# A two-layer diffusion backbone on one core: layer 1's modulation and gate sums four at a time on column groups of TensorE, taps and small vectors laid out by the host

## The chip, the cores and the metric

The kernel runs on one core of one Trainium2 chip (trn2). The metric is the device time of one execution in microseconds. Before the change three runs gave 1686.88, 1685.45 and 1686.14 us; their median is 1686.14.

The engines are named as the profile names them: PE is TensorE (PEld its weight loads), DVE VectorE, ACT ScalarE, POOL GpSimd, SP SyncE, which issues nearly all DMAs. PSUM is the memory that PE writes its results to.

## The reference, cut to what matters

The program is a trunk of two layers over 1024 latent tokens and 256 context tokens of 1024 channels. Layer 0 is windowed attention (16 heads of 128, four key heads), layer 1 a convolution module (a depthwise convolution of 31 taps over 2048 channels between two projections). Both layers are modulated by a conditioning vector `c`:

```python
for i in range(DEPTH):
    shift, scale, gate = jnp.split((silu_c @ ada_w[i] + ada_b[i])[:, None, :], 3, axis=-1)
    h_lat = modulate(rmsnorm(x, norm_g[i]), shift, scale)      # h * (1 + scale) + shift
    ...
    x = x + gate * y                                           # y: attention or convolution branch
return rmsnorm(x, final_g)
```

`silu_c @ ada_w[i]` is a product of one row of 1024 with a matrix of 1024 x 3072. Layer 0's shift and scale are needed at the very start. Layer 0's gate is needed when the attention's output projection ends, layer 1's shift and scale just behind that, layer 1's gate at the end of the kernel. The change touches these four pieces of 1024 values (called chunks of 256 below), and how the depthwise taps `conv_dw_w` (31 x 2048), the biases and the norm weights come into the layout of one channel per partition.

## The kernel before, in words

All large products are made from float32 values split into a high and a low part (`Hh`/`Hl`, `whi`/`wlo`), three matmuls for one product. Weights come as raw tiles of 128 columns (`wraw`), ACT copies the high part, POOL or DVE subtracts it to get the low part.

**Stages.** A start (to about 60 us) loads x, normalizes it, makes layer 0's shift and scale (`ada_mm`, `ada_row`, `ada_cols`, lines 402 to 430) and projects the first key, query and value chunk. The heads follow: a loop over 16 heads x 8 blocks of 128 queries (line 1280). One step computes the scores of the next block, does twelve matmuls of the projections as filler (`fill`), and transposes the probabilities of the present block on PE (`transposes`, line 1119), four or five 128x128 transpositions; every four blocks the product with the values follows. Then come layer 0's output projection, layer 1's projections with the convolution beside them on DVE, ACT and POOL, the layer norm, and layer 1's output projection.

**What sets the order.** PE's instructions are kept in the order in which the program is written (`pin`, line 106 and 1260); the other engines' instructions are put in order by a scheduler that simulates the program. SP's queue of DMAs is one of these: a DMA that waits for its target holds up those behind it.

**The modulation that this change touches** is `ada_rest` (lines 665 to 702), a generator that the head loop advances once a step (line 1327). It has 16 chunks of 256 columns: four of layer 0's gate, eight of layer 1's shift and scale, four of layer 1's gate. For each chunk it takes eight steps, in each of which DVE multiplies a raw 128x256 tile of weights by a column of `silu(c)` and adds it to `acc` in PSUM (the bias comes in as a diagonal, `ident` times a column of `abt`). After the eighth, DVE copies `acc` to `acc_a`, a quarter of the mask's page. One step later PE sums over the 128 partitions: for a gate chunk one fp32 matmul of `ones[:, 0:1]` with `acc_a` (a row of 256, copied by DVE and stored to DRAM, `gd`), for a shift or scale chunk two fp32 matmuls of `acc_a` with a column of ones (two columns of 128, copied to `mod1`). The raw tiles alternate between two places that the taps `dww` and their pair sums `wsum` take later (line 652).

**Taps and small vectors.** `k_rows` (line 173) holds `c`, `c_ctx`, a norm weight and layer 0's biases as 48 rows of 128; PE transposes them once (line 334), and from the result ACT makes `cs = silu(c)`. `k_vecs` holds 128 such rows of biases and norm weights, transposed by `turn_vecs` (line 512) within the first projection. The taps are loaded as two tiles of 31 rows (`dwr`, line 1351) and turned by 16 small transpositions in four calls of `turn_taps` (line 1356), which stand first in the list `later` and are done in the first two steps of layer 0's output projection; the last call sums the taps by pairs (`sum_taps`).

**Pages.** Nearly all SBUF tiles come from a pool of 45 pages of 4 KB per partition (line 115), each freed page going to the end of the list of free ones and each allocation taking the first (lines 54 to 76). A tile in a page waits until the page's last reader is done. `WStream` (line 214) loads and splits the raw weights in such pages: `split` gives up the raw page, and the next `load` follows.

Of the kernel before, what the change touches and what calls it, by code (L numbers as in the profile page):

```python
# [9 lines left out]
F32 = mybir.dt.float32  # L10
# [84 lines left out]
def backbone_kernel(  # L95
    ctx_stack: ExitStack,
    tc: tile.TileContext,
    x, ctx, ada_w, attn_sink, attn_w_out, conv_dw_w, conv_w_out, final_g,
    k_rows, k_vecs, k_ada, k_win, k_wconv, k_xt,
    k_cos, k_sin, k_mask, k_ident,  # L100
    out,
):
# [9 lines left out]
    hfpool = ctx_stack.enter_context(tc.tile_pool(name="halves", bufs=1))  # L112
    ps = ctx_stack.enter_context(tc.tile_pool(name="ps", bufs=2, space=PSUM))
    dr = ctx_stack.enter_context(tc.tile_pool(name="dr", bufs=1, space=bass.MemoryType.DRAM))
    pg = Pages(pgpool, 45, "page", 1024)
    hp = Pages(hfpool, 6, "half", 528)

    uid = [0]
# [10 lines left out]
    def ps_o(i=None):  # L129
        if i is None:  # L130
            oflip[0] ^= 1
            i = oflip[0]
        return ps.tile([P, 512], F32, tag=f"o{i}", name=nm("pso"), bufs=1)

    def ps_g():
        return ps.tile([P, 512], F32, tag="g", name=nm("psg"), bufs=2)
# [13 lines left out]
    def act(out, in_, func, **kw):  # L150
        return A.activation(out=out, in_=in_, func=func, **kw)
# [18 lines left out]
    ptlo = ctile([P, 22, P], F32R, "ptlo")  # L170

    crow_pg = hp.alloc(F32, None, "crow")
    crow = crow_pg[0:48, 0:P]
    SY.dma_start(out=crow, in_=k_rows)
    SY.dma_start(out=idsel, in_=k_ident)
    G.memset(ones, 1.0)
# [153 lines left out]
        ada_load(kt)  # L330

    cs = ctile([P, 40], F32, "cs")[:, 0:16]
    tp = ps_g()
    PE.transpose(tp[:, 0:48], crow, ident[0:48, 0:48])
    act(cs, tp[:, 0:16], AF.Silu)
    V.tensor_copy(vt[:, 96:112], tp[:, 16:32])
    bcol = ctile([P, 16], F32, "bcol")
    V.tensor_copy(bcol[:, 0:8], tp[:, 32:40])
    V.tensor_scalar(out=bcol[:, 8:16], in0=tp[:, 40:48], scalar1=1.0, scalar2=None, op0=ALU.add)
    hp.free(crow_pg)  # L340
    xs1 = load_rows(x[0, 512:768], 2)
    ada_load(6)
    xs1 += load_rows(x[0, 768:1024], 2)
    ada_load(7)
    cx = load_rows(ctx[0], 2)
    vec_pg = pg.alloc(F32, [P], "vecs")
    SY.dma_start(out=vec_pg, in_=k_vecs)
    xt1 = [pg.alloc(F32, [2, 512], "xt") for _ in range(4)]
    for i in range(4):
        SY.dma_start(out=xt1[i], in_=k_xt[i])  # L350
# [158 lines left out]
                PE.matmul(acc[n], w[p // 2][:, kt], (Hl if p == 1 else Hh)[kt][:, sl],  # L509
                          start=kt == 0 and p == 0, stop=kt == KT - 1 and p == 2)  # L510

    def turn_vecs():
        tp = ps_o()
        PE.transpose(tp[:, 0:P], vec_pg, ident)
        V.tensor_copy(vt[:, 0:96], tp[:, 0:96])
        V.tensor_copy(abt, tp[:, 96:P])
        pg.free(vec_pg)

    abt = ctile([P, 32], F32, "abt")

    sa, sb = ps_s(), ps_s()
    acc0 = [t[:, i * 512:i * 512 + 512] for t, i in ((sb, 0), (sb, 1), (sa, 0))]

# [49 lines left out]
    for kt in range(2, KT):  # L573
        nx = kt + 1
        if 2 < kt < KT - 1:
            ada_row(nx)
            tp = turn(xs0, nx, ps_g) if nx < KT - 1 else turn_apart(xs0[0:2], nx, ps_g())
        if kt == 5:
            root1 = rstd_root(ss1, D, 4)
        if kt == KT - 1:  # L580
            x_mm(kt - 1, 0, acc0, (2,))
            turn_vecs()
            for n in (2, 0, 1):
                x_mm(kt, 0, acc0, (n,), (0,))
        x_mm(kt, 0, acc0, (0,), {2: (0,), KT - 1: (1, 2)}.get(kt, range(3)))
        if nx == KT - 1:
            tp = tp, turn_apart(xs0[2:4], nx, ps_o(0))
        if nx < KT:
            ada_cols(nx)
            if kt == 5:  # L590
                r1 = rstd_end(root1, 4)
            if nx < KT - 1:
                x_tile(tp, nx, 0, V)
            else:
                x_tile_apart(tp, nx)
        else:
            x_h(0)
            x_f(1)
            x_l(0)
            rc = rstd_end(rootc, 2)  # L600
        if kt == 2:
            x_mm(kt, 0, acc0, (0,), (1, 2))
        if nx < KT:
            x_mm(kt, 0, acc0, (1,))
            x_mm(kt - 1, 0, acc0, (2,), range(3) if kt > 2 else (2,))
        else:
            x_mm(kt, 0, acc0, (2, 1), (1, 2))
        for i in {3: (0, 1), 4: (2, 3)}.get(kt, ()):
            square(xs1[i], ss1[:, i:i + 1], A)
        if kt == 4:  # L610
            pg.free(*xs1)
        if kt == 5:
            rps = ps_o(1)
            for b in range(4):
                PE.matmul(rps[:, b * P:b * P + P], r1[:, b:b + 1].to_broadcast([P, P]), ident, start=True, stop=True)
            rb_pg = pg.alloc(F32, [1024], "rb")
            rb1 = rb_pg[:, 0:512]
            act(rb1, rps, AF.Copy)
            for i in range(2):
                square(cx[i], ssc[:, i:i + 1], A)  # L620
        if kt == 6:
            pg.free(*xs0)
            cos, sin = (pg.alloc(F32, [1024], n) for n in ("cos", "sin"))
            SY.dma_start(out=cos, in_=k_cos)
            SY.dma_start(out=sin, in_=k_sin)
            rootc = rstd_root(ssc, D, 2)
            x_f(0)
# [20 lines left out]

    gd = [dr.tile([1, D], F32, tag=f"gd{i}", name=f"gd{i}") for i in range(2)]
    mod1 = ctile([P, 16], F32, "mod1")  # L650
    acc_a = mask_pg[:, 768:1024]
    ada_raw = [cpool.tile([P, n], F32, tag=t, name=t + "_raw", bufs=1)[:, 0:256]
               for t, n in (("dww", NJ * TAPS), ("wsum", NJ * 16))]

# [10 lines left out]
    def ada_rest():  # L665
        todo = [(l, c0) for l, c0 in [(0, 2048 + 256 * i) for i in range(4)] + [(1, 256 * i) for i in range(12)]]
        todo = [(l, c0, kt) for l, c0 in todo for kt in range(KT)]

        def load(i):
            l, c0, kt = todo[i]  # L670
            SY.dma_start(out=ada_raw[i % 2], in_=ada_w[l, kt * P:(kt + 1) * P, c0:c0 + 256])

        load(0)
        bank = ps_o(1)
        acc, o = bank[:, 0:256], bank[:, 256:512]
        for i, (l, c0, kt) in enumerate(todo):
            if i + 1 < len(todo):
                load(i + 1)
            raw = ada_raw[i % 2]
            if kt == 0:  # L680
                after(V.tensor_scalar(out=acc, in0=raw, scalar1=cs[:, kt:kt + 1], scalar2=None, op0=ALU.mult))
                for b in range(2):
                    col = (c0 - 2048 if l == 0 else 1024 + c0) // P + b
                    bs = slice(b * P, b * P + P)
                    stt(acc[:, bs], ident, abt[:, col:col + 1], acc[:, bs], ALU.mult, ALU.add)
            else:
                after(stt(acc, raw, cs[:, kt:kt + 1], acc, ALU.mult, ALU.add))
            yield
            if kt < KT - 1:
                continue  # L690
            V.tensor_copy(acc_a, acc)
            yield "copied"
            if i + 1 == len(todo):
                yield
            if c0 >= 2048:
                PE.matmul(o[0:1], ones[:, 0:1], acc_a, start=True, stop=True)
                V.tensor_copy(acc_a[0:1], o[0:1])
                SY.dma_start(out=gd[l][:, c0 - 2048:c0 - 1792], in_=acc_a[0:1])
            else:
                for b in range(2):  # L700
                    PE.matmul(o[:, b:b + 1], acc_a[:, b * P:b * P + P], ones[:, 0:1], start=True, stop=True)
                V.tensor_copy(mod1[:, c0 // P:c0 // P + 2], o[:, 0:2])

    adag = ada_rest()

# [642 lines left out]
    gbc0.append(gate_rows(0))  # L1348


    dwr = pg.alloc(F32, [1024], "dwr"), pg.alloc(F32, [1024], "dwr")
    for i in range(2):
        G.memset(dwr[i][0:32, :], 0.0)
        SY.dma_start(out=dwr[i][0:TAPS, :], in_=conv_dw_w[0, :, i * 1024:(i + 1) * 1024])

    def turn_taps(q):
        o = ps_o()
        for i in range(4):
            j = q * 4 + i
            PE.transpose(o[:, i * 32:(i + 1) * 32], dwr[j // 8][0:32, (j % 8) * P:(j % 8 + 1) * P], ident[0:32, 0:32])  # L1360
        V.tensor_copy(dww[:, q * 4:q * 4 + 4, :], o[:, 0:128].rearrange("p (a b) -> p a b", b=32)[:, :, 0:TAPS])
        if q == 3:
            pg.free(*dwr)
            sum_taps()

    for q in range(4):
        later.append(lambda q=q: turn_taps(q))


    border = []  # L1370
# [573 lines left out]
def _laid_out(i):  # L1944
    rows = [i["c"], i["c_ctx"], i["norm_g"], i["ada_b"][0, 0:2 * D]]
    vecs = [i["conv_b_in"], i["conv_dw_b"], i["conv_ln_g"], i["conv_ln_b"], i["ada_b"][0, 2 * D:], i["ada_b"][1]]
    ada = i["ada_w"][0, :, 0:2 * D].reshape(2, 4, P, 2, KT, P).transpose(4, 0, 2, 1, 3, 5).reshape(KT, 2, P, 4, 2 * P)
    return {"k_rows": np.concatenate([v.reshape(-1, P) for v in rows]),
            "k_vecs": np.concatenate([v.reshape(-1, P) for v in vecs]),
            "k_ada": ada, "k_win": _columns(i["attn_w_in"][0]), "k_wconv": _columns(i["conv_w_in"][0]),  # L1950
            "k_xt": i["x"][0, 512:].reshape(512, 4, 2, P).transpose(1, 3, 2, 0)}


_INS = ["x", "ctx", "ada_w", "attn_sink", "attn_w_out", "conv_dw_w", "conv_w_out", "final_g"]
_OUTS = [((1, T, D), "float32")]


# [18 lines left out]
```

## Time and profile before

| | before |
|---|---|
| median of three runs | 1686.14 us (1685.45 to 1686.88) |
| span of the profiled execution, first to last instruction | 1684.8 us |
| difference between that span and the median (what lies around it) | 1.3 us |
| PE busy, matmul records | 1675.0 us, 8436 |
| DVE, ACT, POOL busy | 1116.1, 878.8, 871.0 us |
| mean clock granted to TensorE | 0.999 |

The profiled execution's own device time is not listed apart from its span, so sums are made against the span and carried to the median.

How to read it: a line of a timeline gives start, duration, engine, line, operation, output and inputs, sizes and count. Since every instruction goes through one helper, nearly all have the line L89, and tiles tell them apart. The records of PE overlap: the start of one record to the start of the next is the turn that it took, its duration is the time until its result is out. A plain fp32 matmul leaves two records, a transposition or a matmul of rounded fp32 one. An idle time in square brackets stands before the work and names what ended it.

### The profile page before, as it was taken

How to read it: one execution, taken by the hardware profiler on the slowest of the kernel's cores; microseconds unless marked ns; L12 is line 12 of the kernel's file. 1: busy time of each engine (PE TensorE's matmuls, PEld its weight loads, DVE VectorE, ACT ScalarE, POOL GpSimd, SP SyncE). 2: the span in 40 equal slices, each digit the busy share in tenths (PEclk: the TensorE clock that was granted, in tenths of full speed). 3: DMA queues.
4: the chain of work that ended last, by engine and by line, in shares of the span. 5: the costliest groups of instructions: out<-in, count | busy, mean ns of one | idle time of the engine just before them, and what ended most of it. 6: DMA issues, size and time to landing. Idle time of an engine off the chain costs nothing.

```text
span 1684.8 us, 23963 instructions
## 1 busy us (share of the span) xinstructions
PE 1675.0 (99%) x8436; PEld 1413.9 (84%) x8436; DVE 1116.1 (66%) x2131; ACT 878.8 (52%) x1555; POOL 871.0 (52%) x722
## 2 busy tenths in 40 slices
PE   9999999999999999999999999999999999999998
PEld 6888888888888888888888888888888888888886
DVE  5765654566356644566324289999999999868732
ACT  5745543555355543556334365555665654566741
POOL 0256653666366663653001267999898888130400
PEclk9999999999999999999999999999999999999999
DMA  9424443454244443447976522020211202387881
GB/s 387 150 85 153 134 121 95 153 153 141 84 152 144 143 135 98 135 135 251 320 233 228 213 94 91 11 72 17 75 51 51 82 33 80 130 276 241 310 298 50
DMA packets 114776, 244.55 MB, mean 145 GB/s; under 512 B 11626, under 2 KB 36514, under 8 KB 114656
## 3 DMA queue, kind: packets, MB, share of 16 engines
q1 hardware_dynamic: 108576, 233.06, 40.9%
q10 hardware_dynamic: 6080, 9.97, 2.4%
q8 instruction: 66, 1.08, 0.3%
q14 instruction: 54, 0.44, 0.1%
HBM read 190.80 MB, written 41.69 MB: 138 GB/s over the span
## 4 chain that ended last, share of the span: by engine, by line
PE 98%; DVE 0%; DMA 0%; ACT 0%; POOL 0%; issue 0%; ACTq 0%; POOLq 0%
PE psg L89 51%; PE pss L89 26%; PE pso L89 22%; DMA rope_half<-rope_half 0%; POOL rope_half L89 0%; DVE x_page L89 0%; ACT p_page L89 0%; DVE wlo_page L89 0%; ACT pthi L89 0%; ACT rope_half L89 0%; ACT whi_page L89 0%; DVE hf_page L89 0%; DVE hl_page L89 0%; ACT qh_page L89 0%; ACT lhi_page L89 0%
## 5 line engine op out<-in xcount | busy, mean ns | idle before, releaser
L89 POOL TENSOR_TENSOR odd_half<-odd_half,prod_half 128x513 f32<-128x513 f32 (+2 forms) x252 | 314.7, 1257 | 22.6 <-ACT prod_half L89 9.4
L89 POOL TENSOR_TENSOR wlo_page<-wraw_page,whi_page 128x512 fp32r<-128x512 f32 (+1 forms) x104 | 173.0, 1680 | 186.7 <-DVE ql_page L89 72.0
L89 PE MATMUL psg<-hh_page,whi_page 128*128 128x512 f32 x600 | 236.3, 394 | 0.0
L89 PE MATMUL psg<-hl_page,whi_page 128*128 128x512 f32 x600 | 234.4, 391 | 0.0
L89 PE MATMUL psg<-hh_page,wlo_page 128*128 128x512 f32 x600 | 234.0, 390 | 0.0
L89 ACT ACTIVATE prod_half<-ubuf,dww 128x513 f32<-128x513 f32 (+2 forms) x252 | 165.6, 675 | 116.9 <-POOL odd_half L89 113.0
L89 PE MATMUL psg<-h2h_page,whi_page 128*128 128x512 f32 x464 | 181.9, 392 | 0.0
L89 PE MATMUL psg<-h2h_page,wlo_page 128*128 128x512 f32 x464 | 180.6, 389 | 0.0
L89 PE MATMUL psg<-h2l_page,whi_page 128*128 128x512 f32 x464 | 180.6, 389 | 0.0
L89 POOL TENSOR_SCALAR p_page<-p_page,sc 128x640 f32<-128x640 f32 (+1 forms) x128 | 99.6, 779 | 149.5 <-DVE sc L89 131.8
L89 DVE SCALAR_TENSOR_TENSOR pss<-ubuf,dww,pss 128x512 f32<-128x512 f32 (+3 forms) x270 | 172.4, 670 | 0.1
L89 DVE SCALAR_TENSOR_TENSOR pss<-ubuf,wsum,pss 128x512 f32<-128x512 f32 (+3 forms) x270 | 171.7, 671 | 0.2
L89 ACT ACTIVATE p_page<-p_page,sc 128x641 f32<-128x641 f32 (+1 forms) x128 | 102.9, 804 | 98.3 <-DVE sc L89 95.9
L89 ACT ACTIVATE pthi<-pss 128x512 fp32r<-128x512 f32 (+2 forms) x144 | 87.3, 618 | 109.7 <-PE pss L89 99.8
L89 DVE TENSOR_TENSOR ptlo<-pss,pthi 128x512 fp32r<-128x512 f32 (+2 forms) x144 | 101.8, 716 | 61.2 <-ACT pthi L89 59.9
L89 PEld LDWEIGHTS psg<-hh_page,wlo_page 128*128 128x128 f32 x600 | 112.7, 188 | 24.3
L89 PEld LDWEIGHTS psg<-hh_page,whi_page 128*128 128x128 f32 x600 | 112.8, 188 | 19.2 <-ACT hh_page L89 0.3
L89 PEld LDWEIGHTS psg<-hl_page,whi_page 128*128 128x128 f32 x600 | 112.8, 188 | 18.4
L89 ACT ACTIVATE whi_page<-wraw_page 128x1024 fp32r<-128x1024 f32 x88 | 92.6, 1052 | 49.8 <-PE psg L89 21.1
L89 PE MATMUL pso<-h2h_page,whi_page 128*128 128x512 f32 x304 | 118.3, 389 | 0.0
L89 PE MATMUL pso<-h2h_page,wlo_page 128*128 128x512 f32 x304 | 118.3, 389 | 0.0
L89 PE MATMUL pso<-h2l_page,whi_page 128*128 128x512 f32 x304 | 118.3, 389 | 0.0
(262 smaller groups left out, 3992.4 us busy)
## 6 DMA issues: line engine op xcount, KB each, us to landing
wraw_page<-in_k_wconv_dram SPq DMA_DIRECT2D x48, 512.0 KB, 3.3
wraw_page<-in_k_win_dram SPq DMA_DIRECT2D x40, 512.0 KB, 3.6
wo_page<-in_attn_w_out_dram SPq DMA_DIRECT2D x32, 512.0 KB, 6.2
wol_page<-wolA SPq DMA_DIRECT2D x32, 512.0 KB, 8.3
wo_page<-in_conv_w_out_dram SPq DMA_DIRECT2D x32, 512.0 KB, 6.7
wol_page<-wolC SPq DMA_DIRECT2D x32, 512.0 KB, 6.2
rope_half<-rope_half ACTq DMA_DIRECT2D x76, 128.0 KB, 2.4
araw_page<-in_k_ada_dram SPq DMA_DIRECT2D x16, 512.0 KB, 10.1
```

The source lines that it names most:

```text
L89: r = f(*a, **k)
```

## The change

- `k_rows` and `k_vecs` are turned by the host, so that a partition holds one channel: `crow` is loaded as 128 x 48 and used as it is, `vt[:, 0:96]` and `abt` are loaded from `k_vecs` by two DMAs at the place of one. The transposition of `crow`, `turn_vecs` and its two copies go.
- `dww` is loaded by one DMA from `k_taps`, laid out by the host. The two tiles `dwr`, their memsets and loads, and the four calls of `turn_taps` go; `sum_taps` becomes the first entry of `later`.
- `acc_a` becomes a tile of its own with four places of 256 columns, and the page pool has 44 pages instead of 45.
- In `ada_rest` each chunk's `acc` is copied to its place, and PE sums only after every fourth chunk: four fp32 matmuls of 256 columns with `ones[:, 0:32]` on the four 32-column groups of the array (`tile_position`), each giving 32 equal rows. DVE copies the 128 x 256 result to the first place. For a gate four rows are stored to DRAM from there. For shift or scale two 128x128 transpositions follow one step later (`turn_back`), and one copy takes eight columns of them to `mod1`.

```diff
-    pg = Pages(pgpool, 45, "page", 1024)
+    pg = Pages(pgpool, 44, "page", 1024)
...
-    crow = crow_pg[0:48, 0:P]
+    crow = crow_pg[:, 0:48]
...
-    tp = ps_g()
-    PE.transpose(tp[:, 0:48], crow, ident[0:48, 0:48])
-    act(cs, tp[:, 0:16], AF.Silu)
+    act(cs, crow[:, 0:16], AF.Silu)
...
-    vec_pg = pg.alloc(F32, [P], "vecs")
-    SY.dma_start(out=vec_pg, in_=k_vecs)
+    abt = ctile([P, 32], F32, "abt")
+    SY.dma_start(out=vt[:, 0:96], in_=k_vecs[:, 0:96])
+    SY.dma_start(out=abt, in_=k_vecs[:, 96:P])
...
-            turn_vecs()
...
-    acc_a = mask_pg[:, 768:1024]
+    acc_a = ctile([P, 4, 256], F32, "acc_a")
...
             yield
+            while turn_back:
+                turn_back.pop()()
             if kt < KT - 1:
                 continue
-            V.tensor_copy(acc_a, acc)
+            k = c0 // 256 % 4
+            V.tensor_copy(acc_a[:, k], acc)
             yield "copied"
             if i + 1 == len(todo):
                 yield
+            if k < 3:
+                continue
+            for k in range(4):
+                PE.matmul(o[32 * k:32 * k + 32], ones[:, 0:32], acc_a[:, k], start=True, stop=True,
+                          tile_position=(0, 32 * k))
+            rows = acc_a[:, 0]
+            V.tensor_copy(rows, o)
+            c0 -= 768
             if c0 >= 2048:
-                PE.matmul(o[0:1], ones[:, 0:1], acc_a, start=True, stop=True)
-                V.tensor_copy(acc_a[0:1], o[0:1])
-                SY.dma_start(out=gd[l][:, c0 - 2048:c0 - 1792], in_=acc_a[0:1])
+                for k in range(4):
+                    SY.dma_start(out=gd[l][:, k * 256:k * 256 + 256], in_=rows[32 * k:32 * k + 1])
             else:
-                for b in range(2):
-                    PE.matmul(o[:, b:b + 1], acc_a[:, b * P:b * P + P], ones[:, 0:1], start=True, stop=True)
-                V.tensor_copy(mod1[:, c0 // P:c0 // P + 2], o[:, 0:2])
+                def back(c0=c0):
+                    for b in range(2):
+                        PE.transpose(o[:, b * P:b * P + P], rows[:, b * P:b * P + P], ident)
+                    V.tensor_copy(mod1[:, c0 // P:c0 // P + 8].rearrange("p (k b) -> p k b", b=2),
+                                  o.rearrange("p (b k n) -> p k b n", b=2, k=4)[:, :, :, 0])
+
+                turn_back.append(back)
...
-    dwr = pg.alloc(F32, [1024], "dwr"), pg.alloc(F32, [1024], "dwr")
-    for i in range(2):
-        G.memset(dwr[i][0:32, :], 0.0)
-        SY.dma_start(out=dwr[i][0:TAPS, :], in_=conv_dw_w[0, :, i * 1024:(i + 1) * 1024])
...
-    for q in range(4):
-        later.append(lambda q=q: turn_taps(q))
+    SY.dma_start(out=dww, in_=k_taps)
+    later.append(lambda: sum_taps())
...
-    return {"k_rows": np.concatenate([v.reshape(-1, P) for v in rows]),
-            "k_vecs": np.concatenate([v.reshape(-1, P) for v in vecs]),
+    return {"k_rows": np.concatenate([v.reshape(-1, P) for v in rows]).T,
+            "k_vecs": np.concatenate([v.reshape(-1, P) for v in vecs]).T,
+            "k_taps": i["conv_dw_w"][0].reshape(TAPS, NJ, P).transpose(2, 1, 0),
```

More of the change, by code (lines that the diff above doesn't have):

```diff
@@ L97, in backbone_kernel @@
     tc: tile.TileContext,
-    x, ctx, ada_w, attn_sink, attn_w_out, conv_dw_w, conv_w_out, final_g,
-    k_rows, k_vecs, k_ada, k_win, k_wconv, k_xt,
+    x, ctx, ada_w, attn_sink, attn_w_out, conv_w_out, final_g,
+    k_rows, k_vecs, k_taps, k_ada, k_win, k_wconv, k_xt,
     k_cos, k_sin, k_mask, k_ident,
@@ L332, in backbone_kernel @@
     cs = ctile([P, 40], F32, "cs")[:, 0:16]
-    tp = ps_g()
-    PE.transpose(tp[:, 0:48], crow, ident[0:48, 0:48])
-    act(cs, tp[:, 0:16], AF.Silu)
-    V.tensor_copy(vt[:, 96:112], tp[:, 16:32])
+    act(cs, crow[:, 0:16], AF.Silu)
+    V.tensor_copy(vt[:, 96:112], crow[:, 16:32])
     bcol = ctile([P, 16], F32, "bcol")
-    V.tensor_copy(bcol[:, 0:8], tp[:, 32:40])
-    V.tensor_scalar(out=bcol[:, 8:16], in0=tp[:, 40:48], scalar1=1.0, scalar2=None, op0=ALU.add)
+    V.tensor_copy(bcol[:, 0:8], crow[:, 32:40])
+    V.tensor_scalar(out=bcol[:, 8:16], in0=crow[:, 40:48], scalar1=1.0, scalar2=None, op0=ALU.add)
     hp.free(crow_pg)
@@ L510, in x_mm @@
                           start=kt == 0 and p == 0, stop=kt == KT - 1 and p == 2)
[L512 to L519, printed above, removed]
     sa, sb = ps_s(), ps_s()
@@ L675, in ada_rest @@
         acc, o = bank[:, 0:256], bank[:, 256:512]
+        turn_back = []
         for i, (l, c0, kt) in enumerate(todo):
@@ L1348, in backbone_kernel @@
     gbc0.append(gate_rows(0))
-    dwr = pg.alloc(F32, [1024], "dwr"), pg.alloc(F32, [1024], "dwr")
-    for i in range(2):
-        G.memset(dwr[i][0:32, :], 0.0)
-        SY.dma_start(out=dwr[i][0:TAPS, :], in_=conv_dw_w[0, :, i * 1024:(i + 1) * 1024])
[L1356 to L1364, printed above, removed]
-    for q in range(4):
-        later.append(lambda q=q: turn_taps(q))
+    SY.dma_start(out=dww, in_=k_taps)
+    later.append(lambda: sum_taps())
     border = []
@@ L1947, in _laid_out @@
     ada = i["ada_w"][0, :, 0:2 * D].reshape(2, 4, P, 2, KT, P).transpose(4, 0, 2, 1, 3, 5).reshape(KT, 2, P, 4, 2 * P)
-    return {"k_rows": np.concatenate([v.reshape(-1, P) for v in rows]),
-            "k_vecs": np.concatenate([v.reshape(-1, P) for v in vecs]),
+    return {"k_rows": np.concatenate([v.reshape(-1, P) for v in rows]).T,
+            "k_vecs": np.concatenate([v.reshape(-1, P) for v in vecs]).T,
+            "k_taps": i["conv_dw_w"][0].reshape(TAPS, NJ, P).transpose(2, 1, 0),
             "k_ada": ada, "k_win": _columns(i["attn_w_in"][0]), "k_wconv": _columns(i["conv_w_in"][0]),
             "k_xt": i["x"][0, 512:].reshape(512, 4, 2, P).transpose(1, 3, 2, 0)}
-_INS = ["x", "ctx", "ada_w", "attn_sink", "attn_w_out", "conv_dw_w", "conv_w_out", "final_g"]
+_INS = ["x", "ctx", "ada_w", "attn_sink", "attn_w_out", "conv_w_out", "final_g"]
 _OUTS = [((1, T, D), "float32")]
```

## Prediction

> **What bounds the kernel now.** I read the page first: the shares of busy time, and the chain that ended last by engine.
>
> ```profile
> span 1684.8 us, 23963 instructions
> PE 1675.0 (99%) x8436; PEld 1413.9 (84%) x8436; DVE 1116.1 (66%) x2131; ACT 878.8 (52%) x1555; POOL 871.0 (52%) x722
> PE 98%; DVE 0%; DMA 0%; ACT 0%; POOL 0%; issue 0%; ACTq 0%; POOLq 0%
> ```
>
> TensorE is busy for 99% of the span and is 98% of the chain. A busy PE can still hide pauses, because a matmul's record covers its whole passage and not only its turn. So I looked next at whom PE waited for, in the view of waits for that engine:
>
> ```profile
> PE pss L89 <- DVE zerr_page L89: 2.0, 1, 2.0
> PE pss L89 <- DVE hl_page L89: 0.2, 1, 0.2
> ```
>
> These two lines are the whole answer: 2.2 us in 1684.8, and 2.0 of it is the wait for the first instruction. No stage is paced by another engine. The rule for this kernel is therefore simple: an instruction taken off TensorE shortens the run by the turn that it took, unless something that was on time by a little now comes late.
>
> How large the turns are is read from starts, not from durations. The groups by line give the counts (a plain fp32 matmul leaves two records, a transposition one):
>
> ```profile
> L89 PE MATMUL pso<-mask_page,ones 128*1 128x256 f32 x16 | 4.7, 377 | 0.0
> L89 PE MATMUL pso<-ones,mask_page 128*128 128x1 f32 x32 | 4.0, 230 | 0.0
> L89 PE MATMUL pso<-ident,dwr_page 32*128 32x32 f32 x16 | 1.4, 224 | 0.0
> ```
>
> That is 8 gate sums (16 records), 16 matmuls of the modulation in 8 events (32 records), and 16 transpositions of taps.
>
> **Part 1, the sums.** The same place of the order exists with and without an event, twice in one stretch of the timeline of PE:
>
> ```profile
> 334.92 0.71 PE L89 MATMUL pss<-ident,p_page 128*128 128x128 f32 x5
> 335.46 0.50 PE L89 MATMUL pso<-ones,mask_page 128*128 128x1 f32 x4
> 335.83 0.36 PE L89 MATMUL pss<-kh_page,qh_page 128*128 128x256 f32 x1
> ...
> 339.15 0.39 PE L89 MATMUL psg<-hh_page,wlo_page 128*128 128x512 f32 x1
> 339.38 0.71 PE L89 MATMUL pss<-ident,p_page 128*128 128x128 f32 x5
> 339.84 0.36 PE L89 MATMUL pss<-kh_page,qh_page 128*128 128x256 f32 x1
> ```
>
> From the first of five transpositions to the next score matmul it takes 0.91 us with a modulation event (335.83 - 334.92) and 0.46 without (339.84 - 339.38). So a modulation event costs 0.45, a transposition in a row of them 0.46 / 5 = 0.09, and an ordinary 512-wide matmul 339.38 - 339.15 = 0.23. The gate event stands in the same place:
>
> ```profile
> 111.09 0.71 PE L89 MATMUL pss<-ident,p_page 128*128 128x128 f32 x5
> 111.73 0.59 PE L89 MATMUL pso<-mask_page,ones 128*1 128x256 f32 x2
> 112.25 0.38 PE L89 MATMUL pss<-kh_page,qh_page 128*128 128x256 f32 x1
> ```
>
> 112.25 - 111.09 - 0.46 = 0.70 us. Removed: 8 x 0.70 + 8 x 0.45 = 9.2 us.
>
> Added are four groups (layer 0's gate, layer 1's shift, scale and gate), each of four fp32 matmuls of 256 columns on 32 columns of the array each, and for shift and scale two transpositions one step later. Such a form runs already in the first stage, in layer 0's modulation, as two rounds of four:
>
> ```profile
> 24.85 0.40 PE L89 MATMUL pss<-hl_page,whi_page 128*128 128x512 f32 x1
> 25.18 1.07 PE L89 MATMUL pso<-araw_page,c_page 128*32 128x256 f32 x16
> 26.18 0.66 PE L89 MATMUL psg<-ident,x_page 128*128 128x128 f32 x4
> ```
>
> 26.18 - 24.85 - 0.23 = 1.10 us for two rounds. One 256-wide fp32 sum by itself costs 0.70 (the gate), so the second round of four added about 0.40, and four side by side take no longer than one. A group should cost what a gate event costs, 0.70; the ends are half of the two rounds, 0.55, and four matmuls behind one another, 0.70 + 3 x 0.40 = 1.9. I take 0.70, the row with the same place in the order and the same single round. Added: 4 x 0.70 + 4 x 0.09 = 3.2 us (2.6 to 8.0). Net of part 1: 9.2 - 3.2 = 6.0 us less.
>
> The Trainium skill (TensorEngine Tiling (Array Packing), Tiling Modes, Key Properties) says that changing the tiling mode drains TensorE, which speaks against the groups. If every entry and every leaving paid a drain of some 0.17 us (an estimate from 398 cycles at 2.4 GHz in TensorE: Matmul & The Clock Gate, Part 2), the four groups would lose 8 x 0.17 = 1.3 us and the whole sum would be 6.8 instead of 8.1.
>
> What lies beside: DVE copies four 128x256 results in place of 8 rows and 8 pairs of columns. DVE is 66% busy and PE waits for it nowhere. In the matmul that closes a group, PE waits for the copy of the fourth chunk, as it does for each chunk now, and one step (4.46 us, 339.38 - 334.92) lies between; the two transpositions of shift and scale come another step after the copy they read. SP issues the same eight gate stores, in two bunches of four: behind them stand loads that are needed a step or more later.
>
> **Part 2, the taps.** Sixteen transpositions in two lots of eight go, and nothing takes their place on PE:
>
> ```profile
> 813.50 0.39 PE L89 MATMUL pss<-woh_page,ozl_page 128*128 128x512 f32 x1
> 813.82 0.68 PE L89 MATMUL pso<-ident,dwr_page 32*128 32x32 f32 x8
> 814.43 0.50 PE L89 MATMUL pss<-woh_page,ozh_page 128*128 128x512 f32 x1
> 814.77 0.40 PE L89 MATMUL pss<-wol_page,ozh_page 128*128 128x512 f32 x1
> ```
>
> From 813.50 to 814.77 there are 1.27 us, of which two ordinary turns are 0.46: 0.81 a lot, 1.6 us for both. The two memsets on POOL, two loads on SP and four copies on DVE go as well and cost nothing now. In their place SP issues one load into the taps' own tile, which must wait for the last read of the raw modulation weights that shared that place; it has the rest of the attention's last head until the taps are summed, and the convolution comes only after layer 0's output projection.
>
> **Part 3, the small vectors.** One transposition between two projection matmuls goes. The chain of waits, in order of time, gives it 0.1 us, and that is the gain (0 to 0.2):
>
> ```profile
> 47.34 0.11 PE pso L89
> ```
>
> **Part 4, the start.** PE's queue holds four warming matmuls, the transposition of the conditioning rows, then 28 more:
>
> ```profile
> 0.74 0.39 SPq L89 DMA_DIRECT2D crow_half<-in_k_rows_dram  x1
> 3.99 0.18 PEld L89 LDWEIGHTS psg<-ident,crow_half 48*128 48x128 f32 x1 [0.65 <-issue]
> 4.26 8.69 PE L89 MATMUL pss<-zerr_page 128*128 128x512 f32 x28
> 4.37 0.18 ACT L89 ACTIVATE cs<-psg 128x16 f32<-128x16 f32 x1 [2.35 <-PE psg L89]
> 11.51 0.70 ACT L89 ACTIVATE dg_half<-ident,r 128x128 f32<-128x128 f32 x2 [0.84 <-DVE r L89]
> 12.88 1.07 PE L89 MATMUL pso<-araw_page,c_page 128*32 128x256 f32 x16
> 13.88 0.94 PE L89 MATMUL psg<-dg_half,x_page 128*128 128x128 f32 x6
> ```
>
> The 28 end at 12.95 and the first real matmuls follow at once, so they are what sets the start. Without the transposition they begin earlier by its own 4.26 - 3.99 = 0.27 and by as much of the 0.65 before it as was a wait: 0.27 to 0.92 at their beginning. At their end it may be less, since early ones run slower than late ones (28 in 8.69 is 0.31 each, an ordinary turn is 0.23), and nothing if a load then sets the pace. I take 0.4 (0 to 0.9).
>
> **Sum.** 6.0 + 1.6 + 0.1 + 0.4 = 8.1 us. The profiled span becomes 1684.8 - 8.1 = 1676.7. The median of the runs shown, 1686.1, stands 1.3 above the span, which is what lies around it; I leave that as it is: 1678.0.
>
> **The rivals.** *Fewer pages make the weights' loads wait (slower).* The page pool shrinks from 45 to 44. Counted along the code, the heads leave as little as one page free after an allocation now, so they leave none then; and 15 of the projection's weight loads would take the very page that their own split has just given up, where now none does. Such a load waits, at the head of SP's queue, until POOL has subtracted the high part. One of the 15 is here, from the views of all engines:
>
> ```profile
> 329.60 0.33 SPq L89 DMA_DIRECT2D wraw_page<-in_k_win_dram  x1
> 331.67 0.33 SPq L89 DMA_DIRECT2D ozd<-oz_half  x1
> 332.75 2.53 POOL L89 TENSOR_TENSOR wlo_page<-wraw_page,whi_page 128x512 fp32r<-128x512 f32 x2
> 336.51 0.80 POOL L89 TENSOR_SCALAR p_page<-p_page,sc 128x640 f32<-128x640 f32 x1
> ...
> 359.65 1.05 ACT L89 ACTIVATE whi_page<-wraw_page 128x1024 fp32r<-128x1024 f32 x1
> ```
>
> It would be issued at 335.3 instead of 329.6, 5.7 us later. The load itself is first read at 359.65, so it is not what would be late. What stands behind it is: a store, which no one needs soon, and the next piece of layer 1's modulation weights, which DVE multiplies in the same queue as the softmax. DVE now loses little to those:
>
> ```profile
>   DMA dww_raw<-in_ada_w_dram: 2.1, 2
> ```
>
> PE has a cover too: the probabilities are scaled by 337.3 and PE turns them at 339.38, 2.1 us later. The rival decides once the delay of a piece passes that cover. If a third of the 15 lost 5.7 - 2.1 = 3.6 us each, that is 18 us and the time 1696. Against it: the next piece's issue often falls after the wait, and SP's order is made with those waits known. I give it 0.07.
>
> *The conditioning comes in late.* Its load goes from 48 rows of 512 B to 128 of 192 B. Now it has landed by 3.99, at most 3.25 after its issue. ACT takes its SiLU before the squares of x, and they lead to the diagonals, ready at 12.21 and used at 13.88 (13.5 if PE is 0.4 earlier): 1.3 us to spare. If it took twice as long, until 7.2, SiLU would be 2.9 later and the first matmuls 1.6 later than in my sum: 1679.6. It decides beyond about 5.7. Chance 0.06. In the Trainium skill (DMA: Bandwidth & Descriptors, Specifications) transfers below 512 B fall short of the line rate by a read-modify-write; no run here shows a row of 192 B.
>
> *The four column groups do not run side by side.* Then a group costs 1.9 and the time is 1678.0 + 4 x 1.2 = 1682.8. Sixteen records in 1.07 us speak against it. Chance 0.04.
>
> *Half is given back elsewhere*, in short waits that a changed order of pages, PSUM banks (the two small ones swap turns once a transposition is gone) and queues brings: about 1684. For it speaks only that PE stands at 99% and any lateness shows; no row names a place. Chance 0.07.
>
> **How the numbers follow.** My forecast has 0.76 and gives 1678.0. A measurement of this kernel tells about 0.2%, 3.4 us, from no change, so faster means below 1682.7. Forecast and late conditioning lie there, 0.82. Groups in a row and the half given back are within 0.2%, 0.11. The page rival is slower, 0.07. For the range: groups at 0.55 and a start of 0.9 give 1.1 less, and the runs spread by 0.7, so it begins at 1676.0. It ends at 1683.0, so that late conditioning and groups in a row are inside.
>
> **What would show it.** In the profile after: the groups named above with `mask_page`, `dwr_page`, `crow_half`, `vecs_page` gone from PE; a new group of 128*32 matmuls with 32 records; from transposition to score matmul about 1.16 us at four places and about 0.64 at two (with two more transpositions), 0.46 elsewhere; the 28 warming matmuls beginning at about 3.7 and the first real ones at about 12.5; PE's waits still about 2 us. I am wrong if PE's waits grow by several us (by SP or DVE in the heads: pages), if a group takes 1.5 us or more, or if the first real matmuls come later than 12.9.

## The result and the profile after

The changed kernel takes 1703.27 us (median; 1702.72 to 1705.48), the kernel before 1686.51 us beside it (1685.45 to 1687.03): the ratio is 1.0103 with a 95% interval of 1.0088 to 1.0117. It became slower by 1%, where 1678.0 was forecast. Below are the same three lines of the page that were read first for the kernel before.

```profile
span 1700.9 us, 23893 instructions
PE 1674.2 (98%) x8406; PEld 1412.0 (83%) x8406; DVE 1120.7 (66%) x2115; ACT 881.4 (52%) x1555; POOL 868.4 (51%) x720
PE 92%; DMA 3%; issue 1%; POOL 1%; ACT 1%; DVE 1%; SPq 0%; ACTq 0%; POOLq 0%; DVEq 0%
```

TensorE (PE) still looks 98% busy, but it was 98% of the chain that ended last and is 92% now; transfers, POOL, ACT and DVE have entered. The view of PE's waits (us in total, times, longest) says whom it waits for:

```profile
PE pss L89 <- DVE sc L89: 4.5, 2, 4.2
PE pss L89 <- POOL p_page L89: 3.2, 2, 1.9
PE pso L89 <- DVE r L89: 2.5, 1, 2.5
PE pss L89 <- POOL ql_page L89: 2.4, 2, 1.4
...
PE pss L89 <- DVE ptlo L89: 1.7, 1, 1.7
PE pso L89 <- ACT vf_half L89: 1.5, 1, 1.5
```

There were two waits before, 2.2 us in all; these six rows alone hold 15.8 us. None of them names a TensorE form that the change touched. They are the softmax (`sc`, `p_page`), the low part of its turned probabilities (`ptlo`), the queries (`ql_page`), the context's values (`vf_half`) and layer 1's norm (`r`).

What the change does on PE came out as forecast. The timeline of PE at the first group of four:

```profile
225.92 0.71 PE L89 MATMUL pss<-ident,p_page 128*128 128x128 f32 x5
226.56 0.64 PE L89 MATMUL pso<-acc_a,ones 128*32 128x256 f32 x8
227.13 0.38 PE L89 MATMUL pss<-kh_page,qh_page 128*128 128x256 f32 x1
...
335.54 0.71 PE L89 MATMUL pss<-ident,p_page 128*128 128x128 f32 x5
336.00 0.36 PE L89 MATMUL pss<-kh_page,qh_page 128*128 128x256 f32 x1
```

From transposition to score matmul it is 1.21 us with a group (227.13 - 225.92), the same at all four groups, and 0.46 where a modulation event has gone (336.00 - 335.54): a group costs 0.75, as against 0.70 forecast. So the sums came out nearly as cheap as forecast, and something else cost about three times what the whole change was to save: 25.3 us lie between 1678.0 and 1703.27.

**Where the waits come from.** The chain of waits, in order of time, at the largest cluster (start, length in us, what):

```profile
375.00 2.54 POOL wlo_page L89 x2
...
377.56 0.33 SPq L89
...
377.99 4.52 DMA low_page<-in_attn_w_out_dram
...
382.54 0.04 ACT lhi_page L89
...
383.13 5.12 DMA rope_half<-rope_half
...
389.71 0.70 POOL p_page L89
```

Read upward, for the last of the cluster's three pauses (388.58 to 390.46): PE waits for probabilities that POOL scales late, since POOL stood at a rotary product whose swapped halves came late; ACT issued that transfer late, since in its order it first had to round a low part (`lhi_page`) that was still on its way; and SP asked for that low part late, since the load of raw weights ahead of it in its queue waited until POOL had split the page (`wlo_page`). The second cluster, from the timeline of all engines:

```profile
574.68 0.33 SPq L89 DMA_DIRECT2D wolC<-low_page  x1
...
580.92 0.75 DVE L89 CUSTOM_DVE_ANT_1 p_page<-pss,mask_page,nsink 128x512 f32<-128x512 f32 x1 [2.45 <-DMA wolC<-low_page]
...
581.83 0.36 PE L89 MATMUL pss<-kh_page,qh_page 128*128 128x256 f32 x1 [4.17 <-DVE sc L89]
...
582.98 0.69 POOL L89 TENSOR_SCALAR p_page<-p_page,sc 128x512 f32<-128x512 f32 x1 [5.04 <-DVE sc L89]
```

Here no weights' load is in the way. A probability tile was given the page of a low part whose store to DRAM had only just been issued, and the softmax waits for that store to land, from its issue at 574.68 until 580.9. PE stands 4.2 us for it. Both clusters look like pages that come round too soon. What the pool's last page is worth, which way it costs, and what else is in the 16 us were left to the experiments.

### The profile page after: what moved, and what is told of

It is laid out like the page before. It is cut to its first block, busy times and chain, and to the rows that moved or that the text cites. A ratio compares the mean times of both kernels' runs of the same rounds, so it can differ in the third digit from the quotient of the medians.

```text
span 1700.9 us, 23893 instructions
## 1 busy us (share of the span) xinstructions
PE 1674.2 (98%) x8406; PEld 1412.0 (83%) x8406; DVE 1120.7 (66%) x2115; ACT 881.4 (52%) x1555; POOL 868.4 (51%) x720
## 4 chain that ended last, share of the span: by engine, by line
PE 92%; DMA 3%; issue 1%; POOL 1%; ACT 1%; DVE 1%; SPq 0%; ACTq 0%; POOLq 0%; DVEq 0%
PE psg L89 47%; PE pss L89 24%; PE pso L89 20%; DMA rope_half<-rope_half 1%; DMA wo_page<-in_conv_w_out_dram 1%; POOL rope_half L89 1%; DMA araw_page<-in_k_ada_dram 0%; DMA wolC<-low_page 0%; POOL wlo_page L89 0%; DMA low_page<-in_attn_w_out_dram 0%; DMA wolA<-low_page 0%; SPq L89 0%; DVE pso L89 0%; POOL low_page L89 0%; ACT v_page L89 0%
## 5 line engine op out<-in xcount | busy, mean ns | idle before, releaser
L89 POOL TENSOR_TENSOR rope_half<-rope_half,sin_page 128x512 f32<-128x512 f32 x38 | 49.2, 1295 | 155.3 <-DMA rope_half<-rope_half 75.3
L89 ACT ACTIVATE woh_page<-wo_page 128x1024 fp32r<-128x1024 f32 x63 | 66.4, 1056 | 107.2 <-DMA wo_page<-in_conv_w_out_dram 45.3
```

The costliest lines, as they stand in the source:

```text
L89: r = f(*a, **k)
```

## The experiments

Twelve kernels were run. Each is compared with the kernel before on the same chip; the kernel before had medians of 1686.0, 1685.8 and 1685.7 us in the three sets.

**The page alone.** The kernel before, with one number altered:

```diff
-    pg = Pages(pgpool, 45, "page", 1024)
+    pg = Pages(pgpool, 44, "page", 1024)
```

> The kernel before with 44 pages instead of 45 and nothing else. Theory (pages): the change's saving on TensorE is real, about 8 us, and the missing page costs it and some 17 us more; so this kernel is about 25 us slower than before, 1711 (1702 to 1716). Rival (the sums): the groups of four make PE wait for DVE and PSUM; then the page costs nothing and this is 1686.5. Rival (order): any edit reshuffles the queues by chance; then this lies anywhere, and most likely within 5 us of 1686.5.

Measured: 1709.53 us, ratio 1.0138 (1.0121 to 1.0154), span 1707.3. PE's waits are of the same kinds as after the change, with nothing else of it in the kernel (the three largest):

```profile
PE pss L89 <- POOL p_page L89: 3.4, 2, 3.2
PE pss L89 <- DVE sc L89: 3.0, 1, 3.0
PE pso L89 <- DVE r L89: 3.0, 1, 3.0
```

One page of 45 costs 23.5 us (22.5 by the spans). That is what the page theory expected, and more than the whole loss.

**The layout alone, with 45 pages.** Conditioning rows, vectors and taps laid out by the host, the sums as before.

> Only the host's layout of taps, rows and vectors, with the sums as before and 45 pages. Pages: the taps' 1.6 us, the vectors' 0.1 and the start's 1.2 (that is what the first stages of the changed kernel showed) are gained: 1683.6 (1682.5 to 1685). The sums: the same. Order: somewhere else, slower than 1686.5 as likely as not.

Measured: 1686.14 us, ratio 0.9999 (0.9990 to 1.0008). A miss: 2.9 us of gain were expected and none came. The taps gave theirs: the eviction of the last head's gate comes 1.04 us later than before (779.82 against 778.78), and layer 1's first projection, behind the taps, 0.61 earlier (970.69 against 971.30), which makes 1.65. What the start had given was lost again near 75 us, where PE goes from 0.6 us ahead of the kernel before to 0.9 behind it; the run with the bank's turn below comes back to it.

**The sums alone, with 45 pages.** The pool keeps its 45 pages, and the four results are put where there was room:

```diff
-    acc_a = mask_pg[:, 768:1024]
+    acc_n = ctile([P, 256], F32, "acc_n")
...
+    acc_at = [mask_pg[:, 768:1024], acc_n, raw_t[0][:, 256:512]]
...
+            places = acc_at + [raw]
+            V.tensor_copy(places[k], acc)
```

`raw_t[0]` is the taps' tile, made 512 columns wide; `raw` is the weight tile that DVE has just read.

> Only the sums by fours, with 45 pages: the four places are the spare quarter of the mask's page, a new tile of 256 words, the tail of the taps' tile (64 bytes longer) and the raw tile just read. Pages: the 6.0 us of the sums are gained, 1680.5 (1679 to 1682.5). The sums: the loss is here, 1695 to 1705. Order: unclear.

Measured: 1681.06 us, ratio 0.9973 (0.9962 to 0.9984). Part 1 of the forecast said 6.0 us less. The medians give 4.9 (2.7 to 6.4 by the interval); the profiled execution, the fastest of seven, has a span of 1678.1, which is 6.7 shorter than before.

**The whole change, with 45 pages and those places.**

> The whole change with 45 pages, by the same four places. Pages: all of the saving appears, 1677.6 (1676 to 1680). The sums: still about 1703. Order: unclear, but not both this and the two parts near their sums.

Measured: 1680.42 us, ratio 0.9971 (0.9961 to 0.9981). Faster, and short of the expectation by what the layout had not given. Against the changed kernel, with its 1703.3 us, only the page and the results' places differ.

**The weights' loads on their own split's page.** The rival on record named this as the page's mechanism. Here 45 pages stay, and only the 15 loads concerned are made to take that page:

```diff
-        i = self.free_.popleft()
+        i = self.free_.pop() if last else self.free_.popleft()
...
-            r = pg.alloc(F32, [KT, P], "wraw")
+            r = pg.alloc(F32, [KT, P], "wraw", own and len(pg.free_) == 2)
```

`own` is set for the load that follows a split in a job of the heads.

> The kernel before with its 45 pages and its old sums; only the 15 weight loads that would find nothing but their own split's page among 44 are made to take that page here too, while every other allocation keeps its spare page. Theory A (the load that waits for POOL at the head of SP's queue is what costs): most of the 23.5 us that one page cost in the kernel before comes back, 1703 (1697 to 1710), with PE waiting for the scaled probabilities near 380 and 577 us. Theory B (the pages of all kinds come round too soon: stores that must land, low parts, the weights at the layer norm): the 15 loads alone cost little, 1687 (1685 to 1690). In between means both.

Measured: 1686.80 us, ratio 1.0008 (0.9999 to 1.0017). The loads do wait: SP's queue stands for POOL's split 26 times, 80.9 us in all, as against 16 times and 56.1 us in the kernel before. Theory A falls. PE's waits:

```profile
PE pss L89 <- DVE zerr_page L89: 2.0, 1, 2.0
PE pss L89 <- POOL ql_page L89: 0.4, 1, 0.4
```

The loads wait and almost nobody minds, as long as everyone else still has a page in hand. In the chain at 375 us the load was one link; by itself it does not carry the loss.

**The changed kernel with one raw chunk ahead.**

```diff
-    wsA.nraw = 2
+    wsA.nraw = 1
```

> The changed kernel with its 44 pages and one word altered: in the heads the stream of projection weights holds one raw chunk ahead in place of two, which leaves a page free. Theories A and B both expect the loss in the heads to go: 1682 (1679 to 1685), of which the wait near 1484 us, which lies behind the heads, keeps 2 to 3 us. If the weights then come late the time stays over 1690, and PE waits for whi or wlo. If neither page theory holds, 1703.

Measured: 1688.21 us, ratio 1.0017 (1.0008 to 1.0026). This misses 1682, but 15 of the 23 us between 1703.3 and 1680.4 are back, with 44 pages and all of the change. What stays is in the waits:

```profile
PE pso L89 <- DVE r L89: 2.9, 2, 2.7
PE psg L89 <- DVE zs_page L89: 2.3, 1, 2.3
...
PE pso L89 <- ACT vf_half L89: 1.8, 3, 0.9
PE pss L89 <- POOL p_page L89: 1.0, 1, 1.0
```

The wait for `r` is the layer norm's, where no weight of the heads holds a page; it is the one part that the expectation had priced. `zs_page` it had not, nor `vf_half`, of which more under the banks.

**The second free page for one kind of tile at a time.** In a pool that hands out its oldest free page, one page less means that every tile gets a page freed later. That can be done to one kind alone, in the kernel before with all 45 pages:

```diff
-        i = self.free_.popleft()
+        n = 1 if len(self.free_) > 1 and self.late and name in LATE else 0
+        i = self.free_[n]
+        del self.free_[n]
```

`late` is on during the heads; `LATE` holds the names of the tiles.

Probabilities alone:

> The kernel before, 45 pages, all work done; during the heads the probability tiles alone take the second free page in place of the oldest one, which is the page that they would get in a pool of 44 with the same history. Theory B1 (what costs is a softmax that must wait until its page's last user, a store or a split, has done): most of the loss in the heads comes back, about 1702 (1697 to 1706). Theory B2 (the low parts): no more than 1688. Theory B3 (only several kinds together): 1687 to 1692.

Low parts alone:

> The same, with the second free page for the low parts' tiles (raw pairs and the rounded halves) alone. Theory B2 (their loads come late, ACT and POOL wait for them in order and the rotary DMAs and probabilities stand behind): about 1702 (1697 to 1706). B1: no more than 1688. B3: 1687 to 1692.

Projection weights alone:

> The same, with the second free page for all tiles of the projection weights (raw, high and low), which is more than the 15 loads that were put on their own split's page before at a cost of 1.0 us. All theories expect little: 1687 (1686 to 1691); over 1697 the weights' high and low tiles, which were not tried before, would be the cause.

All three:

> The same, with the second free page for the three kinds together (probabilities, low parts, projection weights). B1, B2 and B3 all expect what a pool of 44 costs in the heads: 1709.5 less some 4 us that are lost at the layer norm behind them, 1704 (1698 to 1708). If it stays under 1692, the loss needs the page really gone, and the classes that were left out (queries, keys, gates, shared halves) matter.

Measured: probabilities 1688.43 (ratio 1.0015, 1.0006 to 1.0024), low parts 1694.01 (1.0049, 1.0032 to 1.0065), weights 1690.32 (1.0030, 1.0017 to 1.0043), all three 1702.73 (1.0103, 1.0088 to 1.0118). Against 1685.7 that is 2.7, 8.3 and 4.6 us, 15.6 in sum, and 17.0 together. Theory B1 falls. The low parts came out between B2 (1697 and more) and B3 (1692 at most), so neither holds as it was put. No kind carries it: the low parts cost most, and the three add up to nearly what they cost together. PE's waits with all three (the helper's line is L94 here):

```profile
PE pss L94 <- POOL p_page L94: 3.2, 1, 3.2
PE pss L94 <- DVE sc L94: 3.0, 1, 3.0
...
PE pss L94 <- POOL ql_page L94: 1.9, 2, 1.3
PE pss L94 <- DVE ptlo L94: 1.7, 1, 1.7
```

The kernel still has 45 pages, and it shows the waits of the changed kernel in the heads (`p_page`, `sc`, `ql_page`, `ptlo`). How much it explains is seen from PE's lag, that is, how much later the same matmul starts than in the kernel before. At 779 us of the kernel before, near the end of the heads, the lag is 16.5 us here and 15.1 in the run with the page alone. Behind that it stays as it is with 45 pages, and with 44 it grows by 4.0 us across the output projection (to 19.1) and by 3.5 about the layer norm (to 22.6).

**The turn of the PSUM banks.** The two small banks alternate from tile to tile. Without `turn_vecs` there is one tile less, and every later one has the other bank. One line puts the turn back:

```diff
             x_mm(kt - 1, 0, acc0, (2,))
+            oflip[0] ^= 1
             for n in (2, 0, 1):
```

With the layout alone:

> The host's layout alone with 45 pages, and the turn of the two small PSUM banks advanced by one where the transposition of the vectors was, so that from there on every tile gets the bank that it had before the change. Theory C (the missing gain of the layout is lost at 66 to 82 us, where another bank made the planner put a rope DMA ahead of the eviction of vf on ACT): that order is the old one again, and the layout gives 1.5 to 2 us: 1684.3 (1683.3 to 1685.3). Theory D (the loss there has another cause, or the gain was never there): 1686.1 as without it.

Measured: 1684.14 us, ratio 0.9987 (0.9979 to 0.9996), span 1682.0 where the layout without this line had 1684.5. Theory C holds. The timelines of ACT (with one row of PE), first without the line and then with it:

```profile
74.68 0.47 ACTq L89 DMA_DIRECT2D rope_half<-rope_half  x1
75.20 0.39 ACT L89 ACTIVATE vf_half<-pso 128x256 f32<-128x256 f32 x1 [1.66 <-PE pss L89]
...
75.64 0.44 PE L89 MATMUL pso<-ident,vf_half 128*128 128x128 f32 x2 [1.00 <-ACT vf_half L89]
```

```profile
73.52 0.39 ACT L89 ACTIVATE vf_half<-pso 128x256 f32<-128x256 f32 x1
...
74.54 0.47 ACTq L89 DMA_DIRECT2D rope_half<-rope_half  x1
```

With the other bank the planner of the order had put the issue of a rotary transfer ahead of the eviction of `vf`. ACT kept that order and stood 1.7 us, and PE 1.0. With the line, the order of the whole program on ACT differs from that of the kernel before in two places only.

The whole change with 45 pages and this line:

> The whole change with 45 pages (the sums' four results in places that were free) and the bank's turn advanced as before: the four column groups and the layout should now add up. Theory C: 1681.1 - 1.8 = 1679 (1678 to 1680). Theory D: 1680.4 as without the turn.

Measured: 1678.60 us (1677.78 to 1679.22), ratio 0.9956 (0.9942 to 0.9970). This is the version to keep; it beats both kernels. Its page and its waits:

```profile
span 1675.9 us, 23863 instructions
PE 1665.3 (99%) x8406; PEld 1408.8 (84%) x8406; DVE 1111.8 (66%) x2115; ACT 882.1 (53%) x1555; POOL 869.3 (52%) x720
```

```profile
PE pss L89 <- DVE zerr_page L89: 2.0, 1, 2.0
PE pss L89 <- POOL p_page L89: 0.4, 1, 0.4
```

Besides the first instruction's 2.0 us there is next to no wait left, and PE's busy time is 9.7 us shorter than in the kernel before (1675.0 to 1665.3).

## Why the prediction was wrong

**The step that failed** is the weighing of the page. The sum of parts had no term for going from 45 to 44 pages, and the rival that did was given 0.07. By the spans of the profiled executions, the account is: the parts themselves -8.9 (1684.8 to 1675.9), the page +22.5, the bank's turn +2.5, together +16.1, and the span after is 16.1 longer. That it fits to a tenth is luck: by the medians the same terms are -7.2, +23.5 and +2.0, which makes 18.3 where 16.8 were measured, and the page was priced in the kernel before, not in the changed one. The sign does not hang on that. What the record named as a sign of being wrong came true: PE's waits grew by 16.8 us (2.2 to 19.0).

The price in the rival, 18 us, was near. Its mechanism was not, and by that mechanism its chance came out small. It asked only what stands behind one late load in SP's queue and found a store and a piece of modulation weights. DVE does wait for such pieces in the changed kernel, 3.6 us in all against 2.5 before, but at 214, 347 and 546 us, where PE does not stand. The fifteen loads on their own page cost 1.0 us when tried alone. What the replay along the code also said, one page free at the least before and none after, was the better sign: every kind of tile gets its page sooner after its last user, and the low parts (8.3 us), the weights (4.6) and the probabilities (2.7) each lose by it in the heads, and the output projection and the layer norm lose 7.5 more in the run with the page alone. "SP's order is made with those waits known" was counted against the rival. The order made with 44 pages was in fact the slow one; whether another order would have hidden the waits, and what a 46th page would bring, was not tried.

**Part 1** was right: 6.0 forecast, 4.9 by the medians and 6.7 by the spans with the sums alone; the group cost 0.75 us instead of 0.70, side by side. The rule on draining between tiling modes (the Trainium skill, TensorEngine Tiling (Array Packing), Tiling Modes, Key Properties), which would have made it 1.04 by the estimate on record, does not show here: the group takes 0.05 more than the single sum of the kernel before. The rival "do not run side by side" (1.9) falls.

**Part 2** was right: 1.6 forecast, 1.65 measured.

**Parts 3 and 4.** The start gave more than the 0.4 taken. The timeline of PE after:

```profile
10.96 0.64 PE L89 MATMUL pso<-araw_page,c_page 128*32 128x256 f32 x8
11.82 0.64 PE L89 MATMUL pso<-araw_page,c_page 128*32 128x256 f32 x8 [0.23 <-DMA araw_page<-in_k_ada_dram]
```

The first real matmuls begin 1.9 us earlier than at 12.88, and their second half then waits for its weights, so that a load sets the pace, as the text had allowed. At 41 us PE is 1.2 us ahead in the changed kernel (41.48 to 40.26) and 0.7 to 1.0 in the two with the banks' turn put back. The conditioning did not come in late: ACT's SiLU starts at 2.51 us in place of 4.37, so the rows of 192 B had landed by then. That rival falls too. Part 3's 0.1 was not measured apart.

**Half given back elsewhere** (0.07) named the cause of the second loss, the small banks swapping turns, without a place. It cost 2.0 us by the medians and 2.5 by the spans.

With the page and the bank's turn set right the forecast of 1678.0 stands against 1678.6, a gain of 7.2 us by the medians and 8.9 by the spans where 8.1 was forecast. Parts 1 and 2 held, the start was a little better than its term, and the page, which had no term, alone decided the sign.

## What to carry to other kernels

A pool of buffers handed out in turn has no slack that can be read from "one is still free": taking one away makes every tile's page come round sooner, and in this kernel with its nearly full TensorE all three kinds that were tried paid. So an edit that takes a buffer is a term of the sum, and is cheap to try alone: one number altered in the kernel before told it. A tile that is removed also shifts the turn of every later one; compare the order of each engine before and after, and put the turn back if it moved.

## What the runs showed of the hardware

After a cluster of pauses PE does not go on at its old pace. The view by stretches of the changed kernel has in a row the stretch, its length, the busy time of PE, PEld, DVE, ACT and POOL with their counts, the granted clock, the DMA share and GB/s. The stretch behind the first cluster, in four pieces:

```profile
384.10:387.50 3.40, 3.40 (x11) 2.63 (x10) 1.58 (x6) 1.58 (x5) 0.00 (x0) 0.50 0.83 244
387.50:390.90 3.40, 1.52 (x10) 1.01 (x8) 0.00 (x0) 0.00 (x0) 2.43 (x3) 1.00 0.03 10
390.91:394.30 3.39, 3.39 (x13) 3.00 (x12) 1.98 (x4) 2.76 (x5) 3.39 (x4) 0.50 0.06 15
394.33:397.70 3.37, 3.37 (x17) 2.77 (x16) 0.85 (x2) 1.51 (x4) 2.50 (x3) 1.00 0.44 177
```

The second cluster, and a single wait of 2.5 us behind the heads:

```profile
577.00:582.00 5.00, 0.83 (x7) 0.62 (x6) 1.77 (x4) 2.54 (x7) 0.94 (x1) 1.00 0.90 315
582.00:586.00 4.00, 4.00 (x14) 3.41 (x14) 1.80 (x6) 1.41 (x4) 3.02 (x3) 0.57 0.28 72
...
1484.00:1488.00 4.00, 1.49 (x10) 1.06 (x9) 2.47 (x9) 3.42 (x4) 0.00 (x0) 1.00 0.77 298
1488.00:1492.00 4.00, 4.00 (x21) 3.35 (x21) 3.96 (x8) 2.70 (x4) 1.69 (x2) 1.00 0.17 66
```

In the first and the third of the four pieces PE is busy all the time and does 11 and 13 instructions, where it does 17 in the last: the granted clock is 0.50. The timeline of PE there has the 512-wide matmuls 0.43 us apart instead of 0.23:

```profile
384.49 0.63 PE L89 MATMUL psg<-hl_page,whi_page 128*128 128x512 f32 x1
384.92 0.63 PE L89 MATMUL psg<-hh_page,wlo_page 128*128 128x512 f32 x1
```

So a wait can cost more than its own length. The trace's records of the clock have three such stretches, from 384.08, 390.91 and 582.06 us, each 3.41 us long and each beginning within a microsecond of a pause's end; the kernel before has none until its last matmul is done. Half of these 10.2 us, 5 us, is an estimate of their part in the 25 us between 1678.6 and 1703.3.

Their starts lie on one grid of 3.41 us: 390.91 is two steps behind 384.08, and 582.06 is 58. In the step just ahead of the three falls PE stood idle for 1.83, 1.88 and 3.18 us. The wait of 2.5 us at 1484.8 is cut by the grid into 1.79 and 0.72, and none followed. In all fourteen traces, from the first full clock on, the clock fell behind every step with 2.1 us or more of idle PE and behind none with less than 1.8; of four steps with 1.83 to 1.88 two were followed by a fall. So where a pause lies on the grid counts as well as its size.

The Trainium skill (TensorE: Matmul & The Clock Gate, Part 1) states a half-rate clock after an idle window of about 3.4 us, of windows that run free of the kernel. The length, the spacing of the matmuls and the grid agree with it; that the window must be idle throughout, if it is read so, does not, since 1.83 us of idle PE in a step were enough once.
